# Full 128x128 forms for the small transpositions and products of the samples' heads and of the gates' chain, and a sums' row kept on all partitions

## The chip, the cores and the metric

One core of a Trainium2 chip runs the kernel. The time is device microseconds (us) of that core, the median of a few executions. One further execution was taken by the hardware profiler; every start, duration and wait below is of that execution. Engines: PE is TensorE (PEld its weight loads), DVE is VectorE, ACT is ScalarE, POOL is GpSimd, SP issues most of the DMAs.

## The reference

One decoder step: adaptive norm, one wide input product `h @ w_in`, an mLSTM branch (4 heads of 128) and a sliding-window attention branch (8 heads of 64), two output products, a gate and a last norm. It is done for a prompt of 1024 tokens and for 8 samples of 4 tokens each (32 rows), which bring a stored state. All in f32. The part that the change touches is the mLSTM of both:

```python
def mlstm_chunk(carry, inp):
    C, n, m = carry
    q, k, v, ig, lf = inp
    b = jnp.cumsum(lf, axis=-1)
    dmat = jnp.where(causal, b[..., :, None] - b[..., None, :] + ig[..., None, :], -jnp.inf)
    inter = b + m[..., None]
    m_hat = jnp.maximum(inter, jnp.max(dmat, axis=-1))
    s = jnp.einsum('bhtd,bhsd->bhts', q, k) * jnp.exp(dmat - m_hat[..., None])
    w_inter = jnp.exp(inter - m_hat)
    num = jnp.einsum('bhts,bhse->bhte', s, v) + w_inter[..., None] * jnp.einsum('bhtd,bhde->bhte', q, C)
    ...
    m_new = jnp.maximum(b_last + m, jnp.max(d_end, axis=-1))
    w_end = jnp.exp(d_end - m_new[..., None])
    decay = jnp.exp(b_last + m - m_new)
    C_new = decay[..., None, None] * C + jnp.einsum('bhs,bhsd,bhse->bhde', w_end, k, v)
```

The prompt goes in 8 chunks of 128 tokens, so 4 heads x 8 chunks give 32 rows of gate sums. The samples go as one chunk of 4 tokens each.

## The kernel before

**The stream of PE.** Nearly all of the time PE works through large products: the weights come in tiles of 128x128, split in a high and a low part (`wh`, `wl`, type f32r), the moving side is 384, 288 or 512 tokens wide. Their accumulators carry the names that the views show: `g_aq`, `g_mq`, `g_mk`, `g_mv` (plain jobs of 3 pieces each), then `bx`, `bw`, `by`, `bz` (pairs of jobs, seven block products `1,5,6,2,7,3,4` each; kinds `head_in`, `gate`, `query_gate`, `head_gate`), then `ax` ... `az`, `g_w_mo` and `fo...`. A product on PE is written `out<-in`; an f32 product takes two records (a plain transposition one), an f32r product one.

**The work between.** Everything else (attention units, prompt heads, the gates' chain, the samples) consists of Python generators. They `yield` a lag and the PSUM banks that the next step needs (`"b"`, `"o"`, ...). The class `Side` (line 150) is a planner: `mm` and `tr` (lines 271 to 280) add an assumed cost of each PE instruction to `side.now`, and after each step of a large product `side.tick()` starts those generators whose lag has passed and whose banks are free. So the order of PE is written by these sums, and an instruction more or less on PE shifts the points at which later steps go in. DVE, ACT and POOL follow in an order that a scheduler takes from the program; each works its own queue in order. PSUM tiles come from pools of two buffers (`pg`, `pa`, `pb`, `po`), so a product waits when the last reader of its buffer is late.

**The gates' chain** (`gates`, line 632): sums of the gates per chunk are transposed into `gt4` (32 rows of 128). `rp` (line 680) brings the last column of `cm` and `bT` into a row on one partition. On that row about ten DVE instructions make the chunks' maxima (`d0`, `d1`, `mn`, `mr`). `bq` (lines 702 and 703) are two products that spread the row over 128 partitions and turn 32 of its values into a column; `bcs` is the copy. Further on `fp` transposes a full tile, and `fq` (lines 756 and 757) are two transpositions of 4x32 (`ebs`, `mle`).

**The samples' heads** (`sample_head`, line 1195, one after the other): `stk` are two transpositions of 32 columns (keys, values), `sS` a 32x32 product of keys with queries, `sn` the numerator: 16 records of 32 columns with the state, put on four column quarters (`num[j:j + 32]`), and one product over the 32 sample rows (`mm(num[:NS], et, vn, ...)`, line 1244). `Cs` is then scaled on DVE, and `sU` updates the state. POOL clears small tiles and moves single columns.

`smp` (`Pair.samples`) are 16 products with 32 columns on four column quarters, which come once for each pair of jobs; `ada_ga` are of the same kind. `sc`, `pt` and `oT` are the scores, the transposed probabilities and the output of an attention unit; `tk`, `tv`, `S`, `U`, `n` and `ty` belong to the prompt's heads.

Of the kernel before, what the change touches and what calls it, by code (L numbers as in the profile page):

```python
# [10 lines left out]
F32 = mybir.dt.float32  # L11
# [4 lines left out]
ALU = mybir.AluOpType  # L16
# [8 lines left out]
NS = NB * NT  # L25
T = SEQ + NS
PITCH = 1088
NH = 4
# [145 lines left out]
def body(tc, a):  # L174
    nc = tc.nc
    with ExitStack() as ctx:
        cp = ctx.enter_context(tc.tile_pool(name="cp", bufs=1))
# [10 lines left out]
        def pb(shape, name):  # L188
            return ps.tile(shape, F32, tag="b", bufs=2, name=name)
# [4 lines left out]
        def ht(shape, name, dt=F32):  # L194
            return sp.tile(shape, dt, tag="half", bufs=50, name=name)
# [11 lines left out]
        def in_order(ins, eng="PE"):  # L207
            i = getattr(ins, "ins", ins)
            no_sync(i, [last[eng]] if eng in last else [])
            last[eng] = i  # L210
# [27 lines left out]
        V, S, G = Ordered(nc.vector, "V"), Ordered(nc.scalar, "S"), Ordered(nc.gpsimd, "G")  # L238
# [8 lines left out]
        def stores(src=None):  # L247

            for e in list(due):
                if e[0] <= side.now or (src is not None and e[1].tensor is src):  # L250
                    due.remove(e)
                    issue(*e[1:])

        def dma(out, in_, late=False):
            stores(in_.tensor)
            issue(out, in_, late)
# [14 lines left out]
        def mm(out, lhsT, rhs, start, stop, share=1, more=False):  # L271
            n = int(np.prod(rhs.shape[1:]))
            side.now += max(n, 250) / 2400 if rhs.dtype == F32R else max(n * 4 // share, 128) / 2400
            side.products += 1
            in_order(nc.tensor.matmul(out, lhsT, rhs, start=start, stop=stop, skip_group_check=more))  # L275

        def tr(out, in_, idn):
            side.now += 0.11
            side.products += 1
            in_order(nc.tensor.transpose(out, in_, idn))  # L280
# [47 lines left out]
        ident = cst[:, C_ID:C_ID + 128]  # L328
# [3 lines left out]
        ones = tri[:1]  # L332
# [293 lines left out]
        def gates(gp, zg, bias):  # L626
# [29 lines left out]
            an = cp.tile([128, 36], F32, name="an")  # L656
# [9 lines left out]
            gt4 = ht([128, 4, 128], "gt4")  # L666
            G.memset(gt4[:, 1], 0.0)
            aT, bT, zero, cm = (gt4[:32, i] for i in range(4))
# [6 lines left out]
            V.tensor_copy(bTs, sums[32:36, 128:128 + NS])  # L675
            G.memset(zero, 0.0)
            V.tensor_tensor_scan(cm, zero, aT, NEG, ALU.add, ALU.max)
            yield 15.0, "b"

            rp = pb([128, 128], "rp")  # L680
            mm(rp[:1, 0:32], cm[:, 127:128], ident[:32, :32], start=True, stop=True)
            mm(rp[:1, 32:64], bT[:, 127:128], ident[:32, :32], start=True, stop=True)
            row = cp.tile([1, 64], F32, name="row")
            V.tensor_copy(row, rp[:1, 0:64])
            am, bl = row[:, 0:32], row[:, 32:64]
            d0 = cp.tile([1, 32], F32, name="d0")
            d1 = cp.tile([1, 32], F32, name="d1")
            first = lambda t: t.rearrange("p (h c) -> p h c", c=8)[:, :, 0:1]
# [4 lines left out]
            V.tensor_tensor(d1, d1, bl, op=ALU.add)  # L693
            mn = cp.tile([1, 32], F32, name="mn")
            V.tensor_tensor_scan(mn, d0, d1, 0.0, ALU.add, ALU.max)
            dma(a["m_p"], mn.rearrange("p (h c) -> p h c", c=8)[:, :, 7])
            mr = cp.tile([1, 64], F32, name="mr")
            V.memset(mr[:, 32:33], 0.0)
# [3 lines left out]
            yield 11.0, "b"  # L702
            bq = pb([128, 128], "bq")
            mm(bq[:, 0:64], ones, mr, start=True, stop=True)
            mm(bq[:32, 64:65], mr[:, 32:64], ones[:, 0:1], start=True, stop=True)
            bcs = cp.tile([128, 65], F32, name="bcs")
            V.tensor_copy(bcs[:, 0:64], bq[:, 0:64])
            V.tensor_copy(bcs[:32, 64:65], bq[:32, 64:65])
            mcol = bcs[:32, 64:65]
            V.tensor_scalar(nm, cm, mcol, -1.0, op0=ALU.max, op1=ALU.mult)  # L710
# [5 lines left out]
            wend = cp.tile([128, 32], F32, name="wend")  # L716
            V.tensor_tensor(wend, an[:, 0:32], bcs[:, 0:32], op=ALU.subtract)
            S.activation(wend, wend, AF.Exp)
            dec = cp.tile([128, 32], F32, name="dec")
            V.tensor_tensor(dec, bcs[:, 32:64], bcs[:, 0:32], op=ALU.subtract)  # L720
            S.activation(dec, dec, AF.Exp)
# [20 lines left out]
            dma(a["m_s"], v3(bTs)[:, :, 3])  # L742
            ebs = cp.tile([NH, NS], F32, name="ebs")
            S.activation(ebs, bTs, AF.Exp, scale=-1.0)
            mle = cp.tile([NH, NS], F32, name="mle")
            V.tensor_copy(v3(mle), v3(cms)[:, :, 3:4].to_broadcast((NH, NB, NT)))
# [8 lines left out]
            fq = pb([128, 128], "fq2")  # L755
            tr(fq[:NS, 0:4], ebs, ident[:NH, :NH])
            tr(fq[:NS, 4:8], mle, ident[:NH, :NH])
            fls = cp.tile([NS, 8], F32, name="fls")
            V.tensor_copy(fls, fq[:NS, 0:8])
            wes = cp.tile([NS, 4], F32, name="wes")  # L760
# [243 lines left out]
        ymD = [dp.tile([128, T], F32, name=f"ymD{h}") for h in range(NH)]  # L1004
        qs = cp.tile([128, NH, NS], F32, name="qs")
        ks = cp.tile([128, NH, NS], F32, name="ks")
        vs = cp.tile([128, NH, NS], F32, name="vs")
        gs = cp.tile([128, NH, NS], F32, name="gs")
# [188 lines left out]
        def sample_head(h):  # L1197
            an, sxb, fls, wes = st["an"], st["sxb"], st["fls"], st["wes"]
            z = ht([128, 512], "sz")
            kn = sm([96, 128], "skn", 1, F32R)  # L1200
            vn, et, ns4 = z[:NS, 128:257], z[:NS, 257:289], z[:, 289:418]
            Cs = [ht([128, 3, 129], f"Cs{h}_{i}") for i in range(3)]
            bs = [slice(i, min(i + 3, NB)) for i in (0, 3, 6)]
# [4 lines left out]
            tk = pb([128, 2, 128], f"stk{h}")  # L1208
            tr(tk[:NS, 0], ks[:, h], ident)
            tr(tk[:NS, 1], vs[:, h], ident)  # L1210
            S.copy(kn[0:32], tk[:NS, 0])
# [4 lines left out]
            S_ = po([128, NS], f"sS{h}")  # L1216
            mm(S_[:NS], ks[:, h], qs[:, h], start=True, stop=True)
            V.tensor_tensor(et, sxb[:NS, h, 0], cst[:NS, C_CS:C_CS + NS], op=ALU.add)
# [26 lines left out]
            num = po([128, 129], f"sn{h}")  # L1245
            for b in range(NB):
                j = b % 4 * 32
                mm(num[j:j + 32], qf[:, b * NS:(b + 1) * NS], Cs[b // 3][:, b % 3], start=(b < 4), stop=(b >= 4 and j > 0))
            mm(num[:NS], et, vn, start=False, stop=True)
            S.copy(ns4, num)  # L1250
# [981 lines left out]
        for i, r in enumerate(blocks_of_rows):  # L2232
# [69 lines left out]
            else:  # L2302
# [9 lines left out]
                for f, (y, (c0, n)) in enumerate(zip(Y, parts)):  # L2312
                    r.product(4, y, False, c0, n)
                    c = slice(c0, c0 + n)
# [85 lines left out]
```

## Time and profile before

| | us |
|---|---|
| median of 3 runs (lowest, highest) | 822.43 (821.84, 823.16) |
| the profiled execution, its own time | 821.55 |
| its span, from the first to the last instruction | 819.5 |
| PE busy | 804.0 |
| DVE busy | 603.3 |
| ACT busy | 419.5 |
| POOL busy | 49.9 |

The profiled execution lies 0.88 us under the median, and 2.05 us of it lie outside the span. The mean granted clock of PE is 0.997. In the rows of the timeline the columns are: start, duration, engine, line, operation, `out<-in`, rows*columns of the weights, output and input form, count. Durations of PE overlap, since matmuls are pipelined; what a matmul costs is read from start to start. Lines 220, 275 and 280 are those of helpers, so one goes by the names.

### The profile page before, as it was taken

The page shows a single profiled execution, that of the slowest core. Times are in us where ns is not written, and L with a number is a line of the kernel's source. Part 1 is how long each engine was busy: PE and PEld are TensorE (multiplying, and loading weights), DVE is VectorE, ACT ScalarE, POOL GpSimd, SP SyncE. Part 2 cuts the span into 40 slices and gives each one's busy share as a digit, 9 for nine tenths or more (in the row PEclk, how much of TensorE's full clock was granted, in tenths as well). Part 3 has the DMA queues.
Part 4 walks back from the last instruction along what each step waited for, and adds up shares of the span by engine and source line. Part 5 has one row for each costly group of instructions (what it writes and reads, how often), then busy time and mean ns, then how long its engine had stood idle before and what let it go on. Part 6 is the DMA issues. An engine that isn't in the chain of part 4 may idle for free. (4 is left out here: it accounts for less than half of the span.)

```text
span 819.5 us, 15124 instructions
## 1 busy us (share of the span) xinstructions
PE 804.0 (98%) x5154; PEld 665.4 (81%) x5154; DVE 603.3 (74%) x1520; ACT 419.5 (51%) x1020; POOL 49.9 (6%) x117
## 2 busy tenths in 40 slices
PE   8999999999999999999999999999999999999996
PEld 5779798888788878888888878778888779997775
DVE  5899886745756557475667889898669997876666
ACT  5664356556565564546556655554446652224334
POOL 0220000010000000000001011010002101000000
PEclk9999999999999999999999999999999999999998
DMA  9994757546545414537665685864436689647622
GB/s 353 372 339 138 227 165 227 167 152 210 172 138 178 146 59 159 164 131 259 236 210 149 242 264 186 268 209 143 147 105 206 210 287 394 228 142 277 206 104 109
DMA packets 113474, 165.49 MB, mean 202 GB/s; under 512 B 21185, under 2 KB 55745, under 8 KB 113365
## 3 DMA queue, kind: packets, MB, share of 16 engines
q1 hardware_dynamic: 107172, 152.74, 56.7%
q10 hardware_dynamic: 4752, 7.60, 2.5%
q0 software_dynamic: 1472, 4.20, 1.3%
q8 instruction: 40, 0.66, 0.3%
q14 instruction: 38, 0.30, 0.1%
HBM read 115.51 MB, written 50.00 MB: 202 GB/s over the span
## 5 line engine op out<-in xcount | busy, mean ns | idle before, releaser
L220 ACT ACTIVATE p<-p,nmx 128x256 f32<-128x256 f32 (+1 forms) x64 | 31.1, 486 | 19.1 <-DVE nmx L220 19.0
L220 DVE CUSTOM_DVE_ANT_0 p<-sc,cst,sink 128x256 f32<-128x256 f32 (+1 forms) x64 | 26.1, 463 | 9.1 <-PE sc L275 9.0
L275 PE MATMUL g_aq<-h_h,wh_aq 128*128 128x384 f32 (+1 forms) x96 | 32.4, 337 | 0.2 <-ACT aq L220 0.2
L275 PE MATMUL g_aq<-h_h,wl_aq 128*128 128x384 f32 (+1 forms) x96 | 30.9, 322 | 0.0
L275 PE MATMUL g_aq<-h_l,wh_aq 128*128 128x384 f32 (+1 forms) x96 | 30.9, 321 | 0.0
L275 PE MATMUL g_w_mo<-ym_l,wh_w_mo 128*128 128x384 f32 (+1 forms) x96 | 30.8, 321 | 0.0
L275 PE MATMUL g_w_mo<-ym_h,wh_w_mo 128*128 128x384 f32 (+1 forms) x96 | 30.8, 321 | 0.0
L275 PE MATMUL g_w_mo<-ym_l,wl_w_mo 128*128 128x384 f32 (+1 forms) x96 | 30.8, 321 | 0.0
L220 ACT CAST wosh<-wor 128x512 fp32r<-128x512 f32 x24 | 14.8, 621 | 12.9 <-DVE wor L220 12.9
L220 DVE COPY p<-pt 128x512 f32<-128x512 f32 (+1 forms) x16 | 10.5, 656 | 14.8 <-PE pt L280 14.7
L275 PEld LDWEIGHTS g_aq<-h_h,wh_aq 128*128 128x128 f32 x96 | 18.0, 188 | 2.9 <-issue 1.5
L261 POOL DMA_DIRECT2D oD<-uqv x16 | 8.8, 552 | 179.6 <-ACT uqv L220 164.0
L275 PE MATMUL sc<-ukv,uqv 64*128 64x256 f32 (+1 forms) x128 | 18.0, 390 | 1.0 <-DMA ukv<-kD 1.0
L220 DVE SCALAR_TENSOR_TENSOR tgw_mo<-tgw_mo,g_w_mo 128x384 f32<-128x384 f32 (+1 forms) x24 | 12.4, 519 | 8.6 <-PE g_w_mo L275 7.8
L220 DVE TENSOR_TENSOR wosl<-wor,wosh 128x512 fp32r<-128x512 f32 x24 | 16.5, 686 | 2.7 <-ACT wosh L220 2.5
L275 PEld LDWEIGHTS g_aq<-h_l,wh_aq 128*128 128x128 f32 x96 | 18.1, 188 | 0.0
L275 PEld LDWEIGHTS g_w_mo<-ym_l,wh_w_mo 128*128 128x128 f32 x96 | 18.0, 188 | 0.0
L275 PEld LDWEIGHTS g_w_mo<-ym_h,wh_w_mo 128*128 128x128 f32 x96 | 18.0, 188 | 0.0
L275 PEld LDWEIGHTS g_aq<-h_h,wl_aq 128*128 128x128 f32 x96 | 18.0, 188 | 0.0
L275 PEld LDWEIGHTS g_w_mo<-ym_l,wl_w_mo 128*128 128x128 f32 x96 | 18.0, 188 | 0.0
L220 DVE TENSOR_TENSOR et<-et,S 128x384 f32<-128x384 f32 (+1 forms) x12 | 6.1, 510 | 15.7 <-PE S L275 15.7
L275 PE MATMUL g_mq<-h_h,wh_mq 128*128 128x384 f32 (+1 forms) x48 | 16.7, 349 | 0.3 <-ACT mk L220 0.3
(2068 smaller groups left out, 2818.0 us busy)
## 6 DMA issues: line engine op xcount, KB each, us to landing
early_h<-w_ada SPq DMA_DIRECT2D x8, 512.0 KB
adar_ga<-w_ada SPq DMA_DIRECT2D x16, 256.0 KB
wr_ga<-w SPq DMA_DIRECT2D x16, 256.0 KB
wr_gm<-w SPq DMA_DIRECT2D x16, 256.0 KB
taD<-gt SPq DMA_DIRECT2D x16, 256.0 KB
tmD<-gt SPq DMA_DIRECT2D x16, 256.0 KB
wor<-w_out SPq DMA_DIRECT2D x16, 256.0 KB
tga<-taD SPq DMA_DIRECT2D x16, 256.0 KB
```

The costliest lines, as they stand in the source:

```text
L220: ins = f(*args, **kw)
L261: ins = (eng or nc.sync).dma_start(out, in_)
L275: in_order(nc.tensor.matmul(out, lhsT, rhs, start=start, stop=stop, skip_group_check=more))
```

## The change

The transpositions and products of `sample_head` and of the gates' chain take full weights of 128x128 where they took 32 columns, 1 or 4 columns, or 32 rows:

- `ks`, `vs`, `qs` become parts of one tile `kvq`; `whole(i)` is a 128-column piece of it that begins with the wanted 32 columns. `stk` and `sS` take it, and only 32 rows of their outputs are used.
- The last product of `sn` takes all 128 rows of `z`, of which POOL has cleared those columns first (a memset of 128x161 for each head).
- `rp` takes a column of `gt4` broadcast to 128 columns, so that its result, the row, stands on all 128 partitions; the DVE instructions on `row`, `d0`, `d1`, `mn`, `mr` have 128 partitions instead of one. The two products `bq` and their copies fall away; the column `mcol` is made on DVE by one `tensor_tensor_reduce` against the identity.
- `ebs` and `mle` lie in `gt4[:, 2]`, which is transposed whole, once, instead of two transpositions of 4 rows; POOL clears `gt4[:, 1:4]` in one memset of 128x384 (it was 128x128 and 32x128).

```diff
-            G.memset(gt4[:, 1], 0.0)
+            G.memset(gt4[:, 1:4], 0.0)
...
-            mm(rp[:1, 0:32], cm[:, 127:128], ident[:32, :32], start=True, stop=True)
-            mm(rp[:1, 32:64], bT[:, 127:128], ident[:32, :32], start=True, stop=True)
-            row = cp.tile([1, 64], F32, name="row")
-            V.tensor_copy(row, rp[:1, 0:64])
+            for i in range(2):
+                mm(rp[:, 32 * i:32 * i + 32], gt4[:, 3 - 2 * i, 127:128].to_broadcast((128, 128)), ident[:, 0:32], start=True, stop=True)
+            row = cp.tile([128, 64], F32, name="row")
+            V.tensor_copy(row, rp[:, 0:64])
...
-            bq = pb([128, 128], "bq")
-            mm(bq[:, 0:64], ones, mr, start=True, stop=True)
-            mm(bq[:32, 64:65], mr[:, 32:64], ones[:, 0:1], start=True, stop=True)
-            bcs = cp.tile([128, 65], F32, name="bcs")
-            V.tensor_copy(bcs[:, 0:64], bq[:, 0:64])
-            V.tensor_copy(bcs[:32, 64:65], bq[:32, 64:65])
-            mcol = bcs[:32, 64:65]
+            bcs = cp.tile([32, 33], F32, name="bcs")
+            mcol = bcs[:, 32:33]
+            V.tensor_tensor_reduce(bcs[:, 0:32], mr[:32, 32:64], ident[:32, 0:32], 1.0, 0.0, ALU.mult, ALU.add, accum_out=mcol)
...
-            tr(fq[:NS, 0:4], ebs, ident[:NH, :NH])
-            tr(fq[:NS, 4:8], mle, ident[:NH, :NH])
+            tr(fq, gt4[:, 2], ident)
             fls = cp.tile([NS, 8], F32, name="fls")
-            V.tensor_copy(fls, fq[:NS, 0:8])
+            for i in range(2):
+                V.tensor_copy(fls[:, 4 * i:4 * i + 4], fq[NS * i:NS * i + NS, 0:4])
...
-        qs = cp.tile([128, NH, NS], F32, name="qs")
-        ks = cp.tile([128, NH, NS], F32, name="ks")
-        vs = cp.tile([128, NH, NS], F32, name="vs")
+        kvq = cp.tile([128, 3 * NH, NS], F32, name="kvq")
+        ks, vs, qs = (kvq[:, NH * i:NH * i + NH] for i in range(3))
...
+            G.memset(z[:, 128:289], 0.0)
...
-            tr(tk[:NS, 0], ks[:, h], ident)
-            tr(tk[:NS, 1], vs[:, h], ident)
+            whole = lambda i: kvq[:, i:i + 4].rearrange("p h s -> p (h s)")
+            tr(tk[:, 0], whole(h), ident)
+            tr(tk[:, 1], whole(NH + h), ident)
...
-            mm(S_[:NS], ks[:, h], qs[:, h], start=True, stop=True)
+            mm(S_, whole(h), qs[:, h], start=True, stop=True)
...
-            mm(num[:NS], et, vn, start=False, stop=True)
+            mm(num[:NS], z[:, 257:289], z[:, 128:257], start=False, stop=True)
```

**What it moves.** By the planner's sums three PE instructions less stand in the program (two of `bq`, one of `fq`), and their assumed costs, (256 + 128) / 2400 and 0.11, lower `side.now` by 0.27 of its units. From `bq` on, the places of the steps between the large products shift; after the last samples' head the order is that of before again. Three places on PE follow.

The first samples' head on PE, before: its transpositions `stk` and its product `sS` stand in the middle of a block product `bz` of a `gate` pair.

```order
L275 MATMUL bz<-h_h_402,wh_pgate_5__5355 128x512
L275 MATMUL bz<-h_l_403,wh_pgate_5__5355 128x512
L275 MATMUL bz<-h_h_402,wl_pgate_5__5356 128x512
L280 MATMUL stk_5501<-cst,ks 32x128
L280 MATMUL stk_5501<-cst,vs 32x128
L275 MATMUL sS_5509<-qs,ks 32x32
L275 MATMUL bz<-h_h_402,wh_pgate_5__5355 128x512
```

The same head now, on PE:

```order
L275 MATMUL by<-t3h_1711,wh_pgate_7__5441 128x512
L275 MATMUL by<-t3l_1712,wh_pgate_7__5441 128x512
L275 MATMUL by<-t3h_1711,wl_pgate_7__5442 128x512
L280 MATMUL stk_5583<-cst,kvq 128x128 x2
L275 MATMUL sS_5591<-kvq 128x32
L275 MATMUL bx<-h_h_400,wh_pgate_1__5489 128x512
```

The three instructions have 128 columns, and the head begins 42 large products later, between the products `by` and `bx`.

The numerator of the third samples' head on PE, before: `sn` follows the 16 products `smp` of the pair `query_gate1` directly.

```order
L275 MATMUL smp<-wr_az_0_6400,c_102 32x128
L275 MATMUL smp<-wr_az_1_6402,c_102 32x128
L275 MATMUL sn_6515<-Cs_0_6334,qd 32x129 x3
L275 MATMUL sn_6515<-Cs_1_6335,qd 32x129 x3
L275 MATMUL sn_6515<-Cs_2_6336,qd 32x129 x2
L275 MATMUL sn_6515<-sz 32x129
L275 MATMUL by<-t3h_885,wh_pquery_gate_7__6439 128x512
```

The same numerator now, on PE:

```order
L275 MATMUL bw<-t2h_1391,wh_pquery_gate_6__6578 128x512
L275 MATMUL bw<-t2l_1392,wh_pquery_gate_6__6578 128x512
L275 MATMUL bw<-t2h_1391,wl_pquery_gate_6__6579 128x512
L275 MATMUL sn_6647<-Cs_0_6504,qd 32x129 x3
L275 MATMUL sn_6647<-Cs_1_6505,qd 32x129 x3
L275 MATMUL sn_6647<-Cs_2_6506,qd 32x129 x2
L275 MATMUL sn_6647<-sz 32x129
L275 MATMUL bw<-t2h_1713,wh_pquery_gate_6__6578 128x512
```

It has left the neighbourhood of `smp` and stands by itself inside the product `bw`; the fourth head's numerator has done the same.

The scores `sc` of a late attention unit on PE, before: they stand alone inside a block product of a `head_in` pair, and the transposed probabilities `pt` come 21 large products later.

```order
L275 MATMUL bz<-h_h_402,wh_phead_in_5__2869 128x512
L275 MATMUL bz<-h_l_403,wh_phead_in_5__2869 128x512
L275 MATMUL bz<-h_h_402,wl_phead_in_5__2870 128x512
L275 MATMUL sc_0_0_2978<-ukv,uqv 128x128
L275 MATMUL sc_0_1_2979<-ukv,uqv 128x128
L275 MATMUL sc_0_0_2978<-ukv,uqv 128x256
L275 MATMUL sc_0_1_2979<-ukv,uqv 128x256
```

The same scores now, on PE:

```order
L275 MATMUL bw<-h_h_598,wl_phead_in_3__2891 128x512
L275 MATMUL sc_0_0_2996<-ukv,uqv 128x128
L275 MATMUL sc_0_1_2997<-ukv,uqv 128x128
L275 MATMUL sc_0_0_2996<-ukv,uqv 128x256
L275 MATMUL sc_0_1_2997<-ukv,uqv 128x256
L280 MATMUL pt_6_0_3009<-cst,p_2815 128x128 x4
L280 MATMUL pt_6_1_3015<-cst,p_2816 128x128 x4
L275 MATMUL by<-t4h_887,wh_phead_in_4__2933 128x512
```

Scores of one unit and probabilities of another now stand in one run; at this place of the program both take their tiles from the pool `po`. Before, one such pair stood a little later in the same phase (`sc` and `pt` inside a product `bw`).

More of the change, by code (lines that the diff above doesn't have):

```diff
@@ L675, in gates @@
             V.tensor_copy(bTs, sums[32:36, 128:128 + NS])
-            G.memset(zero, 0.0)
             V.tensor_tensor_scan(cm, zero, aT, NEG, ALU.add, ALU.max)
@@ L680, in gates @@
             rp = pb([128, 128], "rp")
-            mm(rp[:1, 0:32], cm[:, 127:128], ident[:32, :32], start=True, stop=True)
-            mm(rp[:1, 32:64], bT[:, 127:128], ident[:32, :32], start=True, stop=True)
-            row = cp.tile([1, 64], F32, name="row")
-            V.tensor_copy(row, rp[:1, 0:64])
+            for i in range(2):
+                mm(rp[:, 32 * i:32 * i + 32], gt4[:, 3 - 2 * i, 127:128].to_broadcast((128, 128)), ident[:, 0:32], start=True, stop=True)
+            row = cp.tile([128, 64], F32, name="row")
+            V.tensor_copy(row, rp[:, 0:64])
             am, bl = row[:, 0:32], row[:, 32:64]
-            d0 = cp.tile([1, 32], F32, name="d0")
-            d1 = cp.tile([1, 32], F32, name="d1")
+            d0 = cp.tile([128, 32], F32, name="d0")
+            d1 = cp.tile([128, 32], F32, name="d1")
             first = lambda t: t.rearrange("p (h c) -> p h c", c=8)[:, :, 0:1]
@@ L693, in gates @@
             V.tensor_tensor(d1, d1, bl, op=ALU.add)
-            mn = cp.tile([1, 32], F32, name="mn")
+            mn = cp.tile([128, 32], F32, name="mn")
             V.tensor_tensor_scan(mn, d0, d1, 0.0, ALU.add, ALU.max)
-            dma(a["m_p"], mn.rearrange("p (h c) -> p h c", c=8)[:, :, 7])
-            mr = cp.tile([1, 64], F32, name="mr")
+            dma(a["m_p"], mn[0:1].rearrange("p (h c) -> p h c", c=8)[:, :, 7])
+            mr = cp.tile([128, 64], F32, name="mr")
             V.memset(mr[:, 32:33], 0.0)
@@ L716, in gates @@
             wend = cp.tile([128, 32], F32, name="wend")
-            V.tensor_tensor(wend, an[:, 0:32], bcs[:, 0:32], op=ALU.subtract)
+            V.tensor_tensor(wend, an[:, 0:32], mr[:, 0:32], op=ALU.subtract)
             S.activation(wend, wend, AF.Exp)
             dec = cp.tile([128, 32], F32, name="dec")
-            V.tensor_tensor(dec, bcs[:, 32:64], bcs[:, 0:32], op=ALU.subtract)
+            V.tensor_tensor(dec, mr[:, 32:64], mr[:, 0:32], op=ALU.subtract)
             S.activation(dec, dec, AF.Exp)
@@ L742, in gates @@
             dma(a["m_s"], v3(bTs)[:, :, 3])
-            ebs = cp.tile([NH, NS], F32, name="ebs")
+            ebs, mle = gt4[:NH, 2, 0:NS], gt4[:NH, 2, NS:2 * NS]
             S.activation(ebs, bTs, AF.Exp, scale=-1.0)
-            mle = cp.tile([NH, NS], F32, name="mle")
             V.tensor_copy(v3(mle), v3(cms)[:, :, 3:4].to_broadcast((NH, NB, NT)))
```

## The prediction

> **What bounds the kernel now.** I read the page first, then PE's busy time in the stretch in which the order moves, then what PE waited for there, and last the timeline around each edited instruction. Here are the page's first lines and one line of the windows view (start and end; length; busy time of PE, PEld, DVE, ACT, POOL; clock, DMA share, GB/s):
>
> ```profile
> span 819.5 us, 15124 instructions
> PE 804.0 (98%) x5154; PEld 665.4 (81%) x5154; DVE 603.3 (74%) x1520; ACT 419.5 (51%) x1020; POOL 49.9 (6%) x117
> ...
> 104.00:620.00 516.00, 514.40 (x3433) 425.20 (x3433) 362.23 (x968) 282.15 (x736) 29.31 (x86) 1.00 0.56 181
> ```
>
> PE is the bound. Between 104 us, where the first edited products stand, and 620 us, behind the samples' last step, it was busy for 514.40 of 516.00 us, at full clock. So two things can move the time here: what PE's own stream costs from start to start, and the 1.60 us in which it stood idle. The waits view names these:
>
> ```profile
> PE bx L275 <- DVE zt L220: 0.7, 1, 0.7
> PE pt L280 <- DVE mx L220: 0.5, 1, 0.5
> PE g_mq L275 <- ACT mk L220: 0.3, 1, 0.3
> ```
>
> Three waits, together 1.5 us, are nearly all of it. Work on DVE, ACT and POOL is hidden as long as it adds nothing to this list.
>
> **The change part by part.** The cost of a run of small products is read thus: start of the second large product behind it, less start of the last large one ahead of it, less two ordinary steps. A step is 0.23 us at 512 tokens, 0.17 at 384, 0.13 at 288.
>
> *Transpositions and product of a samples' head.* The first head, and for comparison a run of eight full transpositions:
>
> ```profile
> 447.83 0.39 PE L275 MATMUL bz<-h_h,wl_pgate__5356 128*128 128x512 f32 x1
> 448.06 0.27 PE L280 MATMUL stk<-cst,ks 128*32 128x128 f32 x1
> 448.17 0.27 PE L280 MATMUL stk<-cst,vs 128*32 128x128 f32 x1
> 448.37 0.25 PE L275 MATMUL sS<-qs,ks 128*32 128x32 f32 x2
> 448.55 0.50 PE L275 MATMUL bz<-h_h,wh_pgate__5355 128*128 128x512 f32 x1
> 448.88 0.40 PE L275 MATMUL bz<-h_l,wh_pgate__5355 128*128 128x512 f32 x1
> ```
>
> ```profile
> 232.51 0.39 PE L275 MATMUL by<-t4h,wl_phead_in__2962 128*128 128x512 f32 x1
> 232.74 1.03 PE L280 MATMUL pt<-cst,p 128*128 128x128 f32 x8
> 233.85 0.39 PE L275 MATMUL by<-t4l,wh_phead_in__2961 128*128 128x512 f32 x1
> ```
>
> The head's four records cost 448.88 - 447.83 - 0.46 = 0.59 us; the eight full ones 233.85 - 232.51 - 0.46 = 0.88, or 0.11 each, all changes included. Four full records are then 0.44: 0.15 less for a head, 0.60 for four. One sees where it sits: 0.20 from the second `stk` to `sS`, and 0.33 instead of 0.23 behind the first `bz`. [...]
>
> *The numerator.* One that stands alone, and one right behind `smp`:
>
> ```profile
> 459.78 0.39 PE L275 MATMUL by<-t3h,wl_pgate__5541 128*128 128x512 f32 x1
> 460.10 0.65 PE L275 MATMUL sn<-Cs,qd 128*32 128x129 f32 x16
> 460.67 0.40 PE L275 MATMUL sn<-sz 32*32 32x129 f32 x2
> 461.01 0.50 PE L275 MATMUL bx<-h_h,wh_pgate__5572 128*128 128x512 f32 x1
> 461.34 0.40 PE L275 MATMUL bx<-h_l,wh_pgate__5572 128*128 128x512 f32 x1
> ```
>
> ```profile
> 548.56 0.28 PE L275 MATMUL smp<-wr_mz,c 128*32 128x128 f32 x2
> 548.65 0.62 PE L275 MATMUL sn<-Cs,qd 128*32 128x129 f32 x16
> 549.54 0.50 PE L275 MATMUL by<-t3h,wh_pquery_gate__6715 128*128 128x512 f32 x1
> ```
>
> The two 32-row records hold PE for 461.01 - 460.67 = 0.34. [...]
>
> ```profile
> 358.03 0.28 PE L275 MATMUL smp<-wr_gm,c 128*32 128x128 f32 x2
> 358.14 0.28 PE L275 MATMUL smp<-wr_gm,c 128*32 128x128 f32 x2
> 358.35 0.50 PE L275 MATMUL by<-t3h,wh_pgate__4315 128*128 128x512 f32 x1
> ```
>
> A record follows the last on its column quarter after 0.11, and the way back to a full product takes 0.21. Two records in one quarter are 0.22: 0.12 less, 0.48 for four heads.
>
> *The gates' chain.* `bq`, `fq` and `rp`:
>
> ```profile
> 117.28 0.43 PE L275 MATMUL bq<-mr,cst 1*128 1x64 f32 x2
> ...
> 117.79 0.44 PE L275 MATMUL g_aq<-h_h,wh_aq 128*128 128x384 f32 x1
> ```
>
> ```profile
> 147.58 0.33 PE L275 MATMUL g_mk<-h_l,wh_mk 128*128 128x384 f32 x1
> 147.75 0.34 PE L275 MATMUL g_mk<-h_h,wl_mk 128*128 128x384 f32 x1
> 148.02 0.18 PE L280 MATMUL fq<-cst,ebs 4*32 4x4 f32 x1
> ...
> 148.44 0.34 PE L275 MATMUL g_mk<-h_l,wh_mk 128*128 128x384 f32 x1
> ```
>
> ```profile
> 104.10 0.29 PE L275 MATMUL g_aq<-h_h,wl_aq 128*128 128x288 f32 x1
> 104.32 0.27 PE L275 MATMUL rp<-cst,gt 32*1 32x32 f32 x4
> ...
> 104.76 0.30 PE L275 MATMUL g_aq<-h_l,wh_aq 128*128 128x288 f32 x1
> 104.89 0.29 PE L275 MATMUL g_aq<-h_h,wl_aq 128*128 128x288 f32 x1
> ```
>
> `bq` goes: 117.79 - 117.28 = 0.51. `fq` costs 148.44 - 147.75 - 0.34 = 0.35 and becomes one full transposition of 0.11: 0.24 less. `rp` costs 104.76 - 104.10 - 0.26 = 0.40 and becomes four full records, 0.44, so it loses 0.04. For its broadcast weights no row exists; a wider load could cost up to the 0.51 of `bq`, whose weights also spread one row's worth over 128 columns, and I take the 0.04 since the load is as large as that of any full record.
>
> *The order.* Before, two numerators stood behind `smp` and shared its mode: from the last `smp` to `by` 549.54 - 548.56 = 0.98, and without the numerator 0.21, so it cost 0.77. Alone it costs 461.34 - 459.78 - 0.46 = 1.10. Now all four stand alone: 2 x 0.33 = 0.66 lost. Likewise the second four products `ada_ga` are parted from the scores `sc` behind them; I take one way back of 0.21 for that, with ends of 0 and 0.33. Other runs are joined or parted between full-width kinds or keep their kind, which I count at nothing.
>
> *Off PE.* The row's ten DVE instructions on 128 partitions keep their lengths along the row, and two PSUM copies go for one reduction; DVE had 153 us free in the stretch. POOL's four new memsets have 161 columns, where it has a memset of 288:
>
> ```profile
> L220 POOL MEMSET qd<- 128x288 f32 x4 | 1.4, 351 | 0.0
> ```
>
> So each takes less than 0.35, on an engine that was busy for 29 of 516 us. New is that DVE's copy `vn` and the `et` of a head wait for it. Queued behind on DVE is the evacuation of large products, and `stk`'s tile in `pb` is held until `vn` is copied; but the transpositions have to come first anyway, and POOL's queue reaches the memset before them unless it stands behind the column copies `n` of the head before. I count 0, with 4 x 0.35 = 1.4 as the end if POOL comes late each time; a gain is not in it.
>
> Sum on PE: -0.60 - 0.48 - 0.51 - 0.24 + 0.04 + 0.66 + 0.21 = -0.92 us.
>
> *The waits.* The longest, `bx` for `zt`, has this ahead of it on DVE:
>
> ```profile
> 527.90 1.37 DVE L220 TENSOR_TENSOR Cs<-Cs,sxb 128x387 f32<-128x387 f32 x3
> 529.19 0.68 DVE L220 SCALAR_TENSOR_TENSOR zt<-zt,bx 128x512 f32<-128x512 f32 x1
> ```
>
> The three `Cs` are what follows the third head's numerator, and `zt` must read the accumulator that `bx` wants. That numerator now stands in a later product, `bw`, so the 1.37 us are out of `zt`'s way and the 0.7 should go; late next is `zt`'s own tanh, with no wait seen. The 0.5 of `pt` came from a run `sc`, `pt` in which both wait for the tiles of `po`; one such run is there again, so it stays. The 0.3 stays as well. Since most steps in the stretch get new neighbours, I put one new wait of the three's mean, 0.5, beside them: -0.7 + 0.5 = -0.2.
>
> Together -1.1. The profiled execution, 821.55, becomes 820.4; against the median, which lies 0.88 higher, 821.3.
>
> **The rivals.** *All waits go* (the new places suit DVE and ACT better): -0.92 - 1.6 = -2.5, 819.9. For it: three waits in 516 us are few and each hangs on one neighbour. Against: the run `sc`, `pt` is there again.
>
> *Slower, by the two tiles of `po`.* In the `head_in` phase scores, one half of the probabilities, `S`, `U`, `n` and `oT` share these two buffers. Five runs stand closer there than before (`oT`, `pt` and soon `sc`; `sc` with `pt`; `pt` and soon `sc`; `oT` with `pt`; `pt` with `n`). Where DVE frees a tile later than the next product of that pool comes up, PE waits, 0.5 as at `pt`, 0.7 as at `bx`. At all five with 0.7 it would be 3.5, less the 0.5 that was there: -0.92 + 3.0 = +2.1, 824.5. It decides from four or more of the five on. Against it: in that phase before, five attention units put their scores there with one wait.
>
> [...]
>
> **How the numbers follow.** A measurement of this kernel can tell about 0.2%, 1.64 us, from no change. Forecast 0.49: 821.3, which with 0.5 either way on its new wait stays within 0.2%. All waits gone 0.31: 819.9, faster by over 0.2%. The `po` tiles 0.13: 824.5, slower by over that. Narrow forms cheaper 0.07: within. So faster 0.31, same 0.56, slower 0.13. The range takes in the first rival and on top of the forecast the bounds of broadcast, POOL and one wait more, 0.5 + 1.4 + 0.5, and leaves out most of the slower case: 819.8 to 823.8.
>
> **What would show it.** In the profile after: `stk` with `sS` at 0.44 (right) or 0.59 and more (wrong); the two records behind `sn` 0.11 apart with no gap ahead of them; no `bq`; `sn` alone at about 1.0 four times; PE's waits between 104 and 620 us without `zt`, and their sum near 1.4. The prediction is wrong if PE's idle time in that stretch passes 3 us or falls under 0.5, or if full records of the heads cost more than 0.11 each.

## The result, and the profile after

The changed kernel takes 828.08 us in the median of 7 runs (827.12 to 828.94, and one run at 835.35), the kernel before beside it 821.84 (820.89 to 823.16, 7 runs). The ratio is 1.0083, with a 95% interval of 1.0063 to 1.0104: slower by over 0.2%. The profiled execution took 828.39 us, 2.05 of it outside its span as before. The forecast of 821.3 and the range up to 823.8 missed; the side was that of the second rival, at a price higher than its 824.5.

The page's first lines and the windows line of the stretch in which the order moves:

```profile
span 826.3 us, 15117 instructions
PE 805.8 (98%) x5149; PEld 666.8 (81%) x5149; DVE 602.4 (73%) x1521; ACT 418.7 (51%) x1020; POOL 55.7 (7%) x120
...
104.00:620.00 516.00, 510.61 (x3402) 422.09 (x3402) 357.36 (x964) 278.92 (x732) 33.94 (x89) 1.00 0.55 178
```

PE stood idle for 516 - 510.61 = 5.39 us of the stretch instead of 1.60. The waits view of the same stretch says for whom:

```profile
PE S L275 <- DVE C L220: 1.2, 1, 1.2
PE sc L275 <- ACT uqv L220: 1.1, 1, 1.1
PE bw L275 <- ACT bw L220: 0.9, 1, 0.9
PE sc L275 <- DVE p L220: 0.9, 2, 0.7
PE pt L280 <- DVE mx L220: 0.6, 1, 0.6
PE tv L280 <- ACT smps L220: 0.5, 1, 0.5
```

`zt` and `mk` are gone from the list, `pt` for `mx` is still there, and the others are new. Four of the six lines (`S`, `sc` twice, `pt`: 3.9 us) are products that wanted a tile of the pool `po`. The 1.1 at `sc` and 0.7 of the 0.9 belong to one run of small products. Its timeline on PE, with the wait and its releaser in brackets:

```profile
190.52 0.82 PE L280 MATMUL pt<-cst,p 128*128 128x128 f32 x6
191.37 0.44 PE L275 MATMUL oT<-p,ukv 128*64 128x128 f32 x4
191.64 0.82 PE L275 MATMUL oT<-p,uqv 128*64 128x128 f32 x12
193.19 0.70 PE L275 MATMUL sc<-ukv,uqv 64*128 64x256 f32 x2 [0.72 <-DVE p L220]
195.03 1.64 PE L275 MATMUL sc<-ukv,uqv 64*128 64x256 f32 x6 [1.15 <-ACT uqv L220]
196.61 0.69 PE L275 MATMUL g_mq<-h_h,wh_mq 128*128 128x384 f32 x1
197.09 0.52 PE L275 MATMUL g_mq<-h_l,wh_mq 128*128 128x384 f32 x1
197.41 0.52 PE L275 MATMUL g_mq<-h_h,wl_mq 128*128 128x384 f32 x1
```

One half of `pt` and then `oT` fill the two tiles of `po`, and the scores `sc` behind them want both. The first comes free with DVE's copy of `pt`, the second with ACT's copy of `oT`. The two queues at that time, DVE first:

```profile
191.99 0.68 DVE L220 TENSOR_TENSOR wr_mk<-ws,wr_mk 128x512 f32<-128x512 f32 x1
192.59 0.55 DVE L220 COPY p<-pt 128x384 f32<-128x384 f32 x1
```

```profile
192.04 0.51 ACT L220 ACTIVATE p<-p,nmx 128x256 f32<-128x256 f32 x1 [0.51 <-DVE nmx L220]
...
193.62 0.49 ACT L220 ACTIVATE p<-p,nmx 128x256 f32<-128x256 f32 x1
...
194.11 0.60 ACT L220 CAST wh_phead_in__2545<-wr_mk 128x512 fp32r<-128x512 f32 x1
194.62 0.36 ACT L220 COPY uqv<-oT 128x256 f32<-128x256 f32 x1
```

`oT` is done at about 192.5, but ACT has four exponentials of another unit and a cast in its queue and copies it at 194.62. Then comes what no wait shows. The windows behind it (the column after POOL's is the granted clock):

```profile
195.00:196.00 1.00, 0.97 (x5) 0.82 (x6) 0.99 (x4) 0.79 (x2) 0.60 (x1) 0.76 0.82 194
196.00:197.00 1.00, 1.00 (x3) 0.40 (x2) 1.00 (x5) 0.00 (x0) 0.00 (x0) 0.50 0.91 258
197.00:198.00 1.00, 1.00 (x4) 1.00 (x4) 0.97 (x7) 0.15 (x1) 0.00 (x0) 0.50 0.83 217
198.00:199.00 1.00, 1.00 (x5) 1.00 (x5) 0.81 (x2) 1.00 (x6) 0.00 (x0) 0.54 0.98 381
```

After the two waits the clock is halved: for 0.24/0.5 + 1 + 1 + 0.46/0.5 = 3.4 us. A 384-token step takes 0.32 instead of 0.17 (197.09 to 197.41), and 1.7 us are lost. PE counts as busy in them.

The run, read as in the prediction from large step to large step, costs 6.40 us; the same run of 30 small products costs 2.95 where nothing holds it (in e12 below).

Of the span's +6.84 us, 0.3 lie ahead of the stretch and 0.4 behind it. In the stretch it is +3.8 of idle time, +1.7 of clock, -0.9 of PE's own work (the terms follow in the part on the prediction) and a remainder of 1.6. Most of that remainder sits in the same runs: compared with their undisturbed twins they cost more than the idle time in brackets, 0.8 in the run at 190 us (6.40 - 2.95 - 1.9 of idle time, less 0.8 for its part at half clock), 0.7 in the one at 181 us (4.17 against 3.33 in e4, with 0.16 shown), 0.6 around `S`, `tv` and `bw`, less 0.7 that a run of the same kind had hidden in the kernel before (the run of e6 below).

### The profile page after: what moved, and what is told of

It reads as the page before. It is cut to its first block, busy times and chain, and to the rows that moved or that the text cites. A ratio compares the mean times of both kernels' runs of the same rounds, so it can differ in the third digit from the quotient of the medians.

```text
span 826.3 us, 15117 instructions
## 1 busy us (share of the span) xinstructions
PE 805.8 (98%) x5149; PEld 666.8 (81%) x5149; DVE 602.4 (73%) x1521; ACT 418.7 (51%) x1020; POOL 55.7 (7%) x120
## 5 line engine op out<-in xcount | busy, mean ns | idle before, releaser
L275 PEld LDWEIGHTS sc<-ukv,uqv 64*128 64x128 f32 x128 | 11.1, 187 | 8.5 <-issue 2.9
```

## The experiments

The common theory: the forms bring the PE time that was worked out, and the loss comes from the order, at places where the scores meet the tiles of `po`. The rival: the forms themselves, or any new order, cost it.

### e1: all the forms, in the order of before

A helper tells the planner of PE instructions that are no longer there:

```diff
+        def counted(cost, n):
+            side.now += cost
+            side.products += n
...
             yield 11.0, "b"
+            counted(256 / 2400, 1)
+            counted(128 / 2400, 1)
             bcs = cp.tile([32, 33], F32, name="bcs")
...
             tr(fq, gt4[:, 2], ident)
+            counted(0.11, 1)
```

> All edits of the change, but the planner is told the assumed costs of the three PE instructions that fell away (two of bq, one of fq), so that the order of PE is that of before except for those three. Theory order (the loss comes from the places to which the steps moved, the full forms themselves save what was predicted): PE's stream gets cheaper by 0.60 + 0.48 + 0.51 + 0.24 - 0.04 = 1.8 us, the waits stay those of before, so about 820.0 to 820.4 against 821.8 of before. Rival theory forms (POOL's memsets, the row on 128 partitions or the shared tile kvq make DVE, ACT and POOL late, wherever the steps stand): 826 or more.

Measured: 822.17 (821.27 to 822.82, 11 runs) beside 822.07 (27 runs), ratio 0.9997 (0.9988 to 1.0006). That is above the 820.0 to 820.4 expected, and far under the rival's 826. So the forms are not what costs 6 us; the rival falls. On PE they save what was worked out, 0.60 at the heads, 0.53 at the numerators, 0.51 at `bq` and 0.22 at `fq`, less 0.05 at `rp`: 1.8 us, read in this run as in the prediction. They don't reach the end: PE's idle time in the stretch is 1.8 us longer than before (3.42 instead of 1.60). From the waits view of this run, between 104 and 620 us:

```profile
PE bx L275 <- DVE zt L220: 1.3, 1, 1.3
PE pt L284 <- DVE gb L220: 0.7, 1, 0.7
PE g_mq L275 <- ACT aq L220: 0.6, 1, 0.6
...
```

PE came earlier to `bx`, and DVE's `zt` did not: 1.3 instead of 0.7. `gb` and `aq` are new: DVE and ACT now do the chain's next steps earlier (`wend`'s exponential at 113.02 instead of 120.06 us), and the attention unit near it comes later (its first exponential at 118.99 instead of 117.69 us), and behind it ACT's copy `aq`.

### e2: the forms of before, in the order of the change

The same helper with the opposite sign, in the kernel before:

```diff
             bcs = cp.tile([128, 65], F32, name="bcs")
+            counted(-256 / 2400, -1)
+            counted(-128 / 2400, -1)
...
             tr(fq[:NS, 4:8], mle, ident[:NH, :NH])
+            counted(-0.11, -1)
```

> The kernel before, no form edited, but the planner doesn't count those three PE instructions, so that the order of PE is that of the changed kernel (bq and the second fq still run). Theory order: as slow as the change plus the 1.8 us that the forms save, 829 to 830. Rival theory forms: only the lost sharing of modes, +0.9 us, so 822 to 823.

Measured: 827.96 (826.54 to 829.44, 4 runs), ratio 1.0067 (1.0053 to 1.0082). Nothing but the order differs from before, and nearly the whole loss is there: the order costs 5.9 us with the old forms (827.96 - 822.07) and 5.9 us with the new ones (828.08 - 822.17 of e1). The 829 to 830 expected were missed, and two costs of the change are absent here: the wait of `S` and, in the profiled execution, the half clock. The two waits at `sc` are the same to 0.01 us (0.72 and 1.15). Behind them the clock differs:

```profile
196.00:197.00 1.00, 1.00 (x6) 0.67 (x6) 1.00 (x6) 0.04 (x1) 0.24 (x1) 1.00 0.69 256
```

In this profiled execution it stayed at 1.00.

### e3: only the samples' heads, in the order of before

The edits of the heads alone, which leave the planner's sums as they were:

```diff
-            tr(tk[:NS, 0], ks[:, h], ident)
-            tr(tk[:NS, 1], vs[:, h], ident)
+            tr(tk[:, 0], whole(h), ident)
+            tr(tk[:, 1], whole(NH + h), ident)
...
-            mm(S_[:NS], ks[:, h], qs[:, h], start=True, stop=True)
+            mm(S_, whole(h), qs[:, h], start=True, stop=True)
...
-            mm(num[:NS], et, vn, start=False, stop=True)
+            mm(num[:NS], z[:, 257:289], z[:, 128:257], start=False, stop=True)
```

> Only the samples' heads are edited (kvq, whole pieces, POOL's memset, the numerator over 128 rows); nothing that the planner counts changes, so the order is that of before. Theory order: -0.60 - 0.48 = -1.1 us, 820.7. Rival theory forms, with the loss in the heads by POOL or kvq: 824 or more; with the loss in the gates' chain: like theory order.

Measured: 821.24 (820.58 to 822.83, 11 runs), ratio 0.9992 (0.9983 to 1.0001): just inside what can't be told from no change, where 820.7 was expected. The heads' terms are there, but the wait for `zt` grew from 0.7 to 1.3 us, which gives half of them back. PE came earlier to `bx`, and DVE's queue, not PE's, set when it could start.

### e4: the change, with the scores in the pool that was asked for

A unit yields with the bank that its scores will need (line 853) and takes the tiles after it (line 856). Line 1038 changes `sc_bank` from the pool `pa` to `po` in between. A unit that has asked for `"a"` before that line then takes tiles of `po`, for which the planner has kept no room. Before, one unit did so, behind `os` and `pt`; in the changed order there are two, the `sc` at 183.38 and the `sc` at 193.19. The experiment keeps what was asked for; PE's order stays as it is in the change:

```diff
-            yield 12.0, sc_bank[1]
+            pool, need = sc_bank
+            yield 12.0, need
...
-            scs = [sc_bank[0]([128, 2, 256], f"sc{g}_{b0}_{kv}") for kv in range(2)]
+            scs = [pool([128, 2, 256], f"sc{g}_{b0}_{kv}") for kv in range(2)]
```

> The changed kernel, but an attention unit that asked the planner for the banks of pool pa takes its scores from pa, also when the switch to po has come in between; PE's order stays that of the changed kernel. Theory order in its sharper form (the largest part is the run pt, oT, sc at 190 us, whose sc waits 0.7 for DVE's copy of pt and 1.1 for ACT's copy of oT in po, and after which the granted clock is at half for some 3 us): 4 to 5 us faster than the change, 823 to 824. Rival: PE only meets the same late DVE and ACT at its next wait, under 1.5 us faster, 827 or more.

Measured: 824.39 (822.76 to 827.39, 10 runs), ratio 1.0027 (1.0015 to 1.0039). That is 3.7 us less than the change, a little under the 4 to 5 expected. The profiled execution, at 827.39 the slowest of the ten, shows the run at 190 us with no wait left:

```profile
191.95 0.82 PE L275 MATMUL oT<-p,uqv 128*64 128x128 f32 x12
192.70 1.90 PE L275 MATMUL sc<-ukv,uqv 64*128 64x256 f32 x8
194.53 0.44 PE L275 MATMUL g_mq<-h_h,wh_mq 128*128 128x384 f32 x1
```

and the clock stays at 1.00 behind it. Not all of it reached the end, since PE then came earlier to the next places:

```profile
PE S L275 <- DVE C L220: 1.6, 1, 1.6
PE tv L280 <- ACT smps L220: 0.9, 1, 0.9
...
```

`S` went from 1.2 to 1.6 and `tv` from 0.5 to 0.9; `bw` (0.9) and `pt` (0.6) wait as in the change. These four, 4.0 us where before had 1.5 in all, are most of what the list shows of the loss that is left.

Two of them begin with a DMA. In the changed kernel, DVE stood 1.50 us until a DMA that stored `uqv` was done, and came late to `C`, for which `S` waits:

```profile
294.85 0.69 DVE L220 TENSOR_TENSOR mkv<-p,bw 128x512 f32<-128x512 f32 x1 [1.50 <-DMA oD<-uqv]
```

The same DVE instruction stood 1.87 us in e4 and 0.16 in e2, where `S` doesn't wait. ACT stood 4.3 us (4.7 in e4) for a DMA that stored `yt` before it came to `smps`, for which `tv` waits. So these two are not the fault that e4 removes.

### e5: the gates' chain alone

The change without the lines of e3's diff; PE's order is that of the change.

> The changed kernel with the samples' heads as before: only the gates' chain is edited, and PE's order is that of the changed kernel. Theory (the order costs, the forms' own saving is mostly eaten by the next wait): 827.5 to 829, with the waits of 0.7 and 1.15 us near 193 to 195 us and those at S and smps gone, since they came only with the heads' new forms. Rival (the heads' new forms bring waits of their own, S for C and tv for smps, 1.8 us, which are more than they save): 825.5 to 826.5.

Measured: 830.63 (830.28 to 831.37, 4 runs), ratio 1.0113 (1.0099 to 1.0126): slower than the change by 2.5 us, and over what either theory gave. The rival falls: in the changed order the heads' new forms do no harm. `tv` for `smps` is gone as expected, but `S` still waits 1.0 us, so that wait did not come with the heads' forms. Their PE time is 4 x (0.605 - 0.455) + 4 x (1.112 - 0.978) = 1.1 us. The waits at `sc` are again 0.72 and 1.15, but the clock behind them is low for longer:

```profile
195.00:196.00 1.00, 0.52 (x2) 0.50 (x4) 0.96 (x4) 1.00 (x4) 0.16 (x1) 0.65 0.81 178
196.00:199.00 3.00, 3.00 (x11) 2.19 (x8) 2.52 (x13) 0.51 (x2) 0.44 (x1) 0.50 0.93 300
199.00:202.00 3.00, 3.00 (x11) 3.00 (x10) 1.65 (x6) 1.90 (x9) 0.00 (x0) 0.50 0.15 57
202.00:203.00 1.00, 1.00 (x8) 0.74 (x8) 0.00 (x0) 0.00 (x0) 0.00 (x0) 0.93 0.00 0
```

0.7 + 6 + 0.1 = 6.8 us at half, twice that of the change, so 1.7 us more are lost. With the 1.1 this is about the 2.5 between the two. That the other three runs of this kernel fell to the same length is not shown: their mean clocks are low (0.990 to 0.995; the change 0.992 to 0.998), but this profiled execution had another 3.4 us at half clock near its start (24.6 to 28.1 us), which counts in such a mean too.

### e6 and e7: the pool kept, in the order of before

The edit of e4 in the kernel before (e6), and in e1 (e7).

> The kernel before, except that an attention unit takes its scores' tiles from the pool whose room it asked the planner for; PE's order is unchanged. Theory (the switch of the pool hurts wherever a unit has asked before it, and before it was cheap since p's and the scores' products stood apart): the one unit that is hit stands after os and pt near 188 us, and 0.3 to 0.6 us of DVE's copy lie ahead of it there: 821.3 to 821.8 where before gives 822.0. Rival (it only matters in the order of the changed kernel): 822.0, no difference.

> The whole change with the order of before (as in the run with all forms in the old order) and with the scores in the pool that was asked for. Theory: 0.3 to 0.6 us less than that run's 822.2, so 821.6 to 821.9, ratio 0.9990 to 0.9996: still no gain that a measurement tells, because the waits that took the 1.8 us are at other places (aq 0.57, gb 0.70, zt 1.31). Rival (the bank was the place where the forms' gain was lost also in the old order): 820.4.

Measured: e6 821.29 (819.93 to 823.15, 11 runs), ratio 0.9992 (0.9983 to 1.0002); e7 821.70 (820.70 to 822.82, 11 runs), ratio 0.9995 (0.9986 to 1.0004). In both, the run `os`, `pt`, `sc` near 188 us costs 3.09 instead of 3.80 us, 0.7 less, as the theory has it: the same fault stood in the kernel before, with one unit and cheaply. Both medians are inside what can't be told from no change.

### e8: another order, and nothing else

The kernel before, with 0.1 us more on the planner's sum (and no edit of any instruction):

```diff
             bcs = cp.tile([128, 65], F32, name="bcs")
+            counted(0.1, 0)
```

> The kernel before, except that the planner is told 0.1 us more at the chain's products: not one instruction differs in form, only the order of PE. Theory (the order of before is one of those with little waiting, 1.6 us in 516, and any other order draws its waits anew; the changed one drew 6 us): 823 to 827. Rival (the changed order was a single bad draw, by the bank near 190 us): within 0.1% of before, 821.3 to 822.8.

Measured: 821.38 (819.89 to 822.91, 10 runs), ratio 0.9997 (0.9988 to 1.0007). My broader theory, that any new order draws its waits anew and dearly, falls: this order has no worse waits than before, and again one unit that takes the other pool.

### e9 and e10: the whole change, in that kind of order

All edits, with another number for the planner (e9), and the same with the pool kept as in e4 (e10):

```diff
+            counted(0.2, 0)
             bcs = cp.tile([32, 33], F32, name="bcs")
```

> The whole change, with the planner told 0.2 us more behind the chain's sums: another order of PE, in which one unit (not two) takes scores' tiles of po that it asked of the other pool for, and stands behind ost and oT instead of pt and oT. Theory (the changed kernel's loss is the pool's switch at those units, not the new order as such): no wait of over 0.5 us between 180 and 200 us, and 820 to 821.5, ratio 0.997 to 0.9995. Rival (the forms or any new order cost): 824 or more.

> The same order and forms, with the scores in the pool that was asked for. Theory: 0.0 to 0.7 us less than the run beside it, so 819.5 to 821.2; this is the version that may beat both kernels: the forms are worth 1.8 us on PE, and if the waits at aq, gb and zt take them as before, it stays at 821.0 to 821.5. Rival (as with the run beside it): 824 or more.

Measured: e9 820.95 (820.32 to 822.43, 11 runs), ratio 0.9987 (0.9978 to 0.9996); e10 820.46 (819.76 to 822.24, 11 runs), ratio 0.9982 (0.9974 to 0.9991). So the same instructions that took 828.08 take 820.95 with one number of the planner moved by 0.2 us. PE's order in e9 is that of e8 except for the products that the change takes out; between these two the new forms bring 0.4 us, too little to tell. e10 beats both kernels, by 1.5 us over before in the medians. Its waits between 104 and 620 us still hold `bx` for `zt` with 1.3 and `g_mq` for `aq` with 0.6 us.

### e11 and e12: a third order, with two such units again

The same line with -0.3 in the place of 0.2 (e11), and the pool kept besides (e12).

> The whole change, with the planner told 0.3 us less: a third order, in which again two units take po after asking for the other pool, and one of them stands behind pt and oT in one run, as in the changed kernel, some 20 large products earlier. Theory (that combination is what costs): PE waits 1.0 to 2.0 us in that run for the copies of pt and oT, and the time is 824 to 828. Rival (the place in the changed kernel was slow for another reason, such as the exps queued on ACT just there): no wait of over 0.5 us there, 820 to 822.

> The third order with the scores in the pool that was asked for. Theory: the wait behind pt and oT goes, 2 to 4 us less than the run beside it, 820.5 to 824. Rival: the same time as the run beside it, within 0.8 us.

Measured: e11 825.30 (824.68 to 825.71, 4 runs), ratio 1.0040 (1.0024 to 1.0055); e12 822.34 (822.07 to 823.86, 10 runs), ratio 1.0008 (0.9999 to 1.0017). Keeping the pool is worth 3.0 us, as expected, but the wait is not where I expected it. In e11 the scores behind `pt` and `oT` started without one; the next `oT` waited instead:

```profile
192.03 0.33 PE L275 MATMUL g_mq<-h_h,wl_mq 128*128 128x384 f32 x1
194.70 0.88 PE L275 MATMUL oT<-p,uqv 128*64 128x128 f32 x12 [2.33 <-DVE mx L220]
```

The scores now held both tiles of `po`, and DVE read them late:

```profile
190.15 0.93 DVE L220 COPY osm<-ost 64x64 f32<-64x64 f32 x4 [1.88 <-PE ost L284]
...
193.05 0.68 DVE L220 TENSOR_TENSOR hb<-hb,hb 128x512 f32<-128x512 f32 x1
193.75 0.48 DVE L220 CUSTOM_DVE_ANT_0 p<-sc,cst,sink 128x256 f32<-128x256 f32 x1
```

DVE had stood 1.88 us for `ost` and then had its queue to work off. So the shortage is the same, and who pays depends on which engine's queue is behind. e12, without it, is still no faster than before: it waits 1.6 us at `bw` and 1.4 us at `bx` in later phases.

## Why the prediction was wrong, point by point

**What bounds the kernel.** PE, before and after. That was read rightly.

**PE's own terms** came out as worked out. A head:

```profile
462.57 0.39 PE L275 MATMUL by<-t3h,wl_pgate__5442 128*128 128x512 f32 x1
462.80 0.38 PE L280 MATMUL stk<-cst,kvq 128*128 128x128 f32 x2
463.02 0.31 PE L275 MATMUL sS<-kvq 128*128 128x32 f32 x2
463.16 0.48 PE L275 MATMUL bx<-h_h,wh_pgate__5489 128*128 128x512 f32 x1
463.48 0.39 PE L275 MATMUL bx<-h_l,wh_pgate__5489 128*128 128x512 f32 x1
```

463.48 - 462.57 - 0.46 = 0.45 (0.44 forecast). From the first `stk` to `sS` it takes 0.22 (462.80 to 463.02) instead of 0.31 (448.06 to 448.37); the step behind the first large product is 0.32 (463.16 to 463.48) where it was 0.33, so of the two gaps in which the prediction saw the saving only the one ahead of `sS` got smaller. A numerator:

```profile
474.17 0.39 PE L275 MATMUL bz<-h_h,wl_pgate__5639 128*128 128x512 f32 x1
474.49 0.65 PE L275 MATMUL sn<-Cs,qd 128*32 128x129 f32 x16
474.95 0.38 PE L275 MATMUL sn<-sz 128*32 128x129 f32 x2
475.26 0.50 PE L275 MATMUL bz<-h_h,wh_pgate__5638 128*128 128x512 f32 x1
475.60 0.40 PE L275 MATMUL bz<-h_l,wh_pgate__5638 128*128 128x512 f32 x1
```

475.60 - 474.17 - 0.46 = 0.97, all four alone, as forecast. Its last two records begin 0.46 behind the first `sn` (474.49 to 474.95) instead of 0.57 (460.10 to 460.67). Where the prediction has numerators share the mode of `smp`, the rows show the same weights, 128*32, and 0.09 from the last `smp` to `sn` (548.56 to 548.65), while a numerator that stood alone began 0.32 behind a full product (459.78 to 460.10); no run shows more of a mode than such gaps. In the same reading `bq` is gone (0.51), `fq` costs 0.12 (in e1, where it stands alone; 0.11 forecast), `rp` 0.45 (0.44), and the scores that were parted from `ada_ga` 0.21 more (0.21). The sum of -0.92 holds. The chance of 0.07 was for narrow forms that cost less than full ones. That falls: the head's narrow records cost 0.59 and its full ones 0.45, and from the first to the second narrow `stk` it took 0.11 (448.06 to 448.17), as long as a full transposition.

**The broadcast weights of `rp` and POOL's memsets** were counted at nothing, and nothing is seen of them: no wait of PE in the stretch names POOL. A memset of 128x161 takes 0.24 us, and DVE's copy of the row 0.22 on 128 partitions where it was 0.21 on one.

**The waits.** This is the step that failed: "I put one new wait of the three's mean, 0.5, beside them: -0.7 + 0.5 = -0.2." `zt` went, as said; the 0.5 of `pt` stayed, as said (0.6). But the new waits are not one of 0.5: the list sums to 5.3 us where 1.4 was forecast, and PE's idle time, 5.39 us, is past the 3 us that the prediction gave as a sign of being wrong. Nor had the sum a term for the clock (1.7 us) or for what the runs cost beyond the idle time that is shown (1.6 us). A mean over the waits of before says what is left in an order that had none worse; it says nothing of a place that the old order never had.

**The second rival** had the right buffers, but not the place. The waits on tiles of `po` sum to 3.9 us, near the 3.5 that it priced, and that is luck. Its five runs stand in the `head_in` phase, which begins at 206 us in the changed kernel. Of these, `sc` with `pt` waited (0.61 us at 236.30), as one such run had before, and in the run with `n` it was `S` (1.22 us at 295.85), behind a DMA. The other 2.0 us belong to the two units of e4, whose scores stand before that phase, in the last plain job `g_mq`; it named neither. The argument against it was that five units had put their scores in `po` before with one wait. The code shows what this missed (lines 853, 856 and 1038): units that ask for `po` wait until the planner has room there; a unit caught by line 1038 doesn't. e4 and the pair e11 and e12 show its weight, 3.7 us (with the clock's part) and 3.0 us. Its sum had no term for the clock, nor for waits outside of `po` (`bw` 0.9, `tv` 0.5). Two of the prediction's sums are a little off besides: four waits of 0.7 give -0.92 + 2.8 - 0.5 = +1.4, short of the 1.64 from which this rival decides, and the range's upper end is 821.3 + 2.4 = 823.7, not 823.8.

**The first rival**, all waits go, failed on the same step; e3 and e1 show besides that time saved on PE ahead of a fixed queue on DVE is partly paid back there: the wait for `zt` grew from 0.7 to 1.3 us in both. Even in e10 only 1.5 us reach the end: 1.8 of the forms, 0.5 of the pool and 0.3 of `mk`, which doesn't wait there, less 0.6 more at `zt` and 0.6 at `aq`.

**What stays open:** why the clock stayed low for twice as long in e5 (the last section says what the traces show of when it falls); and how the rest of e4's 2.3 us over before divides among its four waits, which no experiment removed one by one.

## What to carry to other kernels

Where a planner writes the order from assumed costs, an edit's own cost and the cost of the order that it brings are two questions: keep the planner's sums as they were and try the new forms in the old order, and the old forms in the new one. Look for resources that are taken later than they are asked for, because a shift of 0.2 us in the order can decide whether one unit or two slip past the reservation. And a saving on the bounding engine is worth only as much as the queues ahead of its next waits let through: in e1 PE's own work got 1.8 us cheaper, and its idle time 1.8 us longer.

## What the hardware showed that was not expected

Behind idle time of 0.72 and 1.15 us within 2.6 us the granted clock halved in two profiled executions and not in a third. With these same two waits at the same place it stayed at 1.00 in e2, was 0.50 for 3.4 us in the changed kernel and for 6.8 us in e5; one idle time of 2.33 us in e11 left it at 1.00.

The traces show part of what differs. In the profiled execution of the changed kernel the first record at full clock begins at 4.36 us, and the clock changes at 195.51, 198.92 and 823.56 us: 56, 57 and 240 steps of 3.41 us later (191.15 / 56 = 3.413). In that of the kernel before it begins at 6.19 us, and the one change, at 815.14, comes 237 such steps later. In the changed kernel both waits lie within one such step (first line; the second is the step behind it); in e2, with the steps counted in the same way, a boundary lies between them (the other two lines):

```profile
192.10:195.51 3.41, 1.54 (x14) 0.88 (x11) 2.24 (x6) 3.41 (x13) 0.12 (x1) 1.00 0.59 178
195.51:198.92 3.41, 3.41 (x13) 2.68 (x10) 3.26 (x14) 1.35 (x6) 0.48 (x1) 0.50 0.88 271
...
190.23:193.64 3.41, 2.48 (x26) 1.97 (x26) 3.15 (x13) 2.06 (x8) 0.00 (x0) 1.00 0.87 219
193.64:197.05 3.41, 2.26 (x12) 1.48 (x12) 2.50 (x10) 2.40 (x8) 0.60 (x1) 1.00 0.80 253
```

PE's idle time is 3.41 - 1.54 = 1.87 us in the first, and 0.93 and 1.15 us in the two of e2. In e5 one step held 1.69 us, and the clock fell; in e11 the 2.33 us were divided into 0.74 and 1.59, and it did not. No other step between 104 and 620 us held more than 1.22 us in the changed kernel or 0.71 in the kernel before, and no other fall was seen there in these two. So, as far as these traces go, equal waits cost 1.7 us more or nothing more by how they lie to those steps. Idle time is not the whole condition: e5's second step at half clock followed one with 0.18 us of it, and from 20 to 40 us the mean clock was 0.91 in e4 and e5, where PE stood idle for 1.27 and 1.21 us, and 1.00 in the changed kernel, where it stood for 1.79.

The weights of `rp`, which repeat one column 128 times, cost no more here than the full ones of `sS`: their loads last 187 to 192 ns in the trace, those of `sS` 189 to 192 (a full transposition's, `fq`, 143), and the four records together cost 0.45 us, 0.11 each.
